# Two Strassen products of eleven blocks computed early and parked in DRAM, in place of four plain blocks

## Chip and metric

One core of one Trainium2 chip. The metric is the device time of one execution in microseconds (us); of several runs, the median. Engines are named as in the profile: PE is TensorE (PEld its weight loads), DVE is VectorE, ACT is ScalarE, POOL is GpSimd, and SP is the queue that issues nearly all DMAs.

## What is computed

One decoder layer on 1024 tokens of width 1024, all in float32: two groups of heads, an output projection, and then a feed-forward part. The change lies in the up-projection of the feed-forward part:

```
h = rms_norm(x, ffn_pre_norm)                          # 1024 x 1024
u = causal_depthwise_conv(h @ w_up, conv_w, conv_b)    # 1024 x 5632, 3 taps over the tokens
u_gate, u_val = split(u)                               # 2 x 2816 columns
y = gelu(u_gate) * u_val
x = x + rms_norm(y @ w_down, ffn_post_norm)
```

## The kernel before

Every float32 matmul is made of three: each operand is split into a high part (a ScalarE copy into a shorter format) and a low part (VectorE takes the difference), and `mm3` (line 121) adds high x high, high x low and low x high into one PSUM bank. A bank is 128 partitions x 512 columns. The tokens are worked on in two halves of 512 (`hh` 0 and 1).

The up-projection has 22 blocks. Block `i` yields 128 gate columns and 128 value columns for all 1024 tokens. Four of them (`AHEAD`) go the plain way: `plain(i, hh)` (line 669) runs 2 x 24 matmuls for each half of the tokens, then the convolution's taps (`taps`, line 660), the gelu and the gate multiply, all 512 wide, and stores the result to `yd` in DRAM. While the plain blocks of the first half run, the second half's residual and norm are made (`post_a`, `post_n`, `post_b`, spread over the units by `interleave`): `post_b` (line 599) transposes the normed rows on TensorE and splits them into `hi` and `lo`. While the plain blocks of the second half run, `tbuild` (line 690) makes the sums of activations T1 to T4 that the other blocks need: it adds high and low parts back together (B), subtracts and splits again.

The other 18 blocks go through Strassen's scheme (`strassen`, line 777): seven products of 12 matmuls instead of eight. Its right operands are T1 to T4 and three quarters of the activations: B11 and B21 (first half of the tokens), B22 (second half). The left operands are made by `prep(i)` (line 729) from the block's weights, loaded into one `raw` tile: four sums on VectorE and seven splits, into the buffers `oh`/`ol` (five each, `split`) and `sh`/`sl` (four each, `ssplit`). The order of products is written out: T1 into bank `PC`, T2 onto bank `PA`, B21 into `PB`, T3 onto `PA`, then `head(i + 1)` (line 770), which opens the next block's `PA` with its B11 product P1, then T4 onto `PA` and B22 onto `PC`. Between the products ScalarE copies `PA` out (`p1`, `u2`, `u3`), and VectorE adds (lines 788, 792, 798) into `ug` and `uv`. `gate(i)` (line 801) then does the taps 1024 wide, the gelu and the multiply, and stores to `yd`.

`prep(i + 1)` stands before `strassen(i)` in the code. A scheduler orders the instructions of each engine when the program is built, by what is ready in its model and by the order in the code; within an engine the result is fixed. `in_turn` (line 94) keeps some of them in the order of the code: the first matmul of every product, and the splits that take a buffer of `oh` or `sh`. Tiles of one tag share a fixed number of buffers: eight of four banks' width for tag T (`ttile`) and eight for tag a (`atile`), four for each of f0 to f3 (`ftile`), two of `xtile`, and three of `u` (`utile`). Four PSUM banks are `big` and four `small`. After the last block the down-projection starts from `load_1` and `feed_1`.

Of the kernel before, what the change touches and what calls it, by code (L numbers as in the profile page):

```python
# [8 lines left out]
F32 = mybir.dt.float32  # L9
# [12 lines left out]
AHEAD = 4  # L22
# [5 lines left out]
def tile_hymba_layer(  # L28
# [61 lines left out]
    yd = dr.tile([NF, P, D], F32, name="yd")  # L90

# [477 lines left out]
    def post_a(hh, b, st):  # L569
        ss = st["ss"][:, b, :]  # L570
        r = norm_cols(ss[:, 0:2], f"post1_{hh}_{b}")
        w = st["wide"]
        tmp = ttile(f"post{hh}_{b}", F32)
        for dh in range(2):
            ds = slice(dh * H, dh * H + H)
            mt = st["m"][b, dh]
            xr = tmp[:, dh, :]
            nc.sync.dma_start(xr, xN[4 * hh + b, :, ds])
            nc.vector.scalar_tensor_tensor(out=mt, in0=mt, scalar=r, in1=w[:, dh, :], op0=ALU.mult, op1=ALU.mult)
            nc.vector.tensor_tensor(out=mt, in0=mt, in1=xr, op=ALU.add)  # L580
        st["h"][b] = tmp

    def post_n(hh, b, st):
        ss = st["ss"][:, b, :]
        w = st["wide"]
        tmp = st["h"][b]
        for dh in range(2):
            ds = slice(dh * H, dh * H + H)
            mt = st["m"][b, dh]
            xr = tmp[:, dh, :]  # L590
            nc.scalar.activation(xr, mt, AF.Square, accum_out=ss[:, 2 + dh : 3 + dh])
            nc.sync.dma_start(x1d[4 * hh + b, :, ds], mt)
        r = norm_cols(ss[:, 2:4], f"pre2_{hh}_{b}")
        for dh in range(2):
            mt = st["m"][b, dh]
            h = tmp[:, 2 + dh, :]
            nc.vector.scalar_tensor_tensor(out=h, in0=mt, scalar=r, in1=w[:, 2 + dh, :], op0=ALU.mult, op1=ALU.mult)

    def post_b(hh, b, st):
        for dh in range(2):  # L600
            ps = small(f"pH{hh}_{b}_{dh}")
            for j in range(4):
                nc.tensor.transpose(ps[:, j * P : j * P + P], st["h"][b][:, 2 + dh, j * P : j * P + P], ident)
            pv = ps.rearrange("p (j q) -> p j q", j=4)
            bs = slice(b * P, b * P + P)
            nc.scalar.activation(st["hi"][dh][:, :, bs], pv, AF.Copy)
            nc.vector.tensor_tensor(
                out=st["lo"][dh][:, :, bs], in0=pv, in1=st["hi"][dh][:, :, bs].bitcast(F32), op=ALU.subtract
            )
# [19 lines left out]
    st_out = []  # L629
    for hh in range(2):  # L630
# [5 lines left out]
        if hh == 0:  # L636
# [7 lines left out]
            def utile(name):  # L644
                return f.tile([P, D], F32, tag="u", name=name, bufs=3)
# [3 lines left out]

            halo = f.tile([P, AHEAD, 2, 2], F32, tag="halo", name="halo")  # L650
            wide = ttile("wide", F32)
            for i in range(2):
                nc.sync.dma_start(wide[:, 2 * i : 2 * i + 2, :], wides[i].rearrange("p (a b) -> p a b", a=2))
# [15 lines left out]
    def plain(i, hh):  # L669
        act = [None, None]  # L670
        for t in range(2):
            b = t * NF + i
            ps = block(w_u[b], act2[hh], f"u{hh}_{i}_{t}")
            u = utile(f"u{hh}_{i}_{t}")
            c0 = 2 * hh
            if hh == 1:
                nc.gpsimd.tensor_copy(u[:, 0:2], halo[:, i, t, :])
            nc.scalar.activation(u[:, c0 : c0 + H], ps, AF.Copy)
            if hh == 0:
                nc.gpsimd.tensor_copy(halo[:, i, t, :], u[:, H - 2 : H])  # L680
            a = ftile(t, f"a{hh}_{i}_{t}")
            taps(a, u, b, c0)
            act[t] = a
        nc.scalar.activation(act[0], act[0], AF.Gelu_apprx_tanh)
        nc.vector.tensor_tensor(out=act[0], in0=act[0], in1=act[1], op=ALU.mult)
        nc.sync.dma_start(yd[i, :, hh * H : hh * H + H], act[0])

    TS = {}

    def tbuild(kt):  # L690
        B = {}
        for n, (hh, k) in (("11", (0, 0)), ("12", (1, 0)), ("22", (1, 1)), ("21", (0, 1))):
            t = ftile(2 + kt % 2, f"B{n}_{kt}")
            hi, lo = act2[hh]
            nc.vector.tensor_tensor(
                out=t, in0=hi[k][:, kt, :].bitcast(F32), in1=lo[k][:, kt, :].bitcast(F32), op=ALU.add
            )
            B[n] = t

        def keep(n, v):  # L700
            if kt == 0:
                TS[n] = (ttile(f"{n}h"), ttile(f"{n}l"))
            h, l = TS[n][0][:, kt, :], TS[n][1][:, kt, :]
            nc.scalar.activation(h, v, AF.Copy)
            nc.vector.tensor_tensor(out=l, in0=v, in1=h.bitcast(F32), op=ALU.subtract)

        def sub(out, x, y, eng):
            eng.tensor_tensor(out=out, in0=x, in1=y, op=ALU.subtract)
            return out

        t1 = sub(B["11"], B["12"], B["11"], nc.vector)
        keep("T1", t1)
        t3 = sub(B["12"], B["22"], B["12"], nc.vector)
        t2 = sub(t1, B["22"], t1, nc.vector)
        keep("T2", t2)
        keep("T3", t3)
        t4 = sub(t2, B["21"], t2, nc.vector)
        keep("T4", t4)

# [9 lines left out]
    def prep(i):  # L729
        if i == AHEAD:  # L730
            raw = [load_w(w_u[t * NF + i], 1024, f"u{i}_{t}") for t in range(2)]
            a11, a12, a21, a22 = [raw[c // 2][:, c % 2 * H : c % 2 * H + H] for c in range(4)]
        else:
            raw = atile(f"raw{i}", F32)
            for t in range(2):
                nc.sync.dma_start(raw[:, 2 * t : 2 * t + 2, :], w_u[t * NF + i].rearrange("p (a b) -> p a b", a=2))
            a11, a12, a21, a22 = [raw[:, c, :] for c in range(4)]
        o = {"B11": split(a11, f"u{i}a11")}
# [29 lines left out]
    heads = {}  # L768

    def head(i):  # L770
        ps = big(f"PA_{i}")
        prod(i, "B11", ps)
        p1 = ftile(2, f"p1_{i}")
        nc.scalar.activation(p1, ps, AF.Copy)
        heads[i] = ps, p1

    def strassen(i):
        pa, p1 = heads.pop(i)
        lo, hi = slice(0, H), slice(H, D)
# [12 lines left out]
        nc.vector.tensor_tensor(out=uv[:, hi], in0=pc, in1=u3, op=ALU.add)  # L792
        if i + 1 < NF:
            head(i + 1)
        prod(i, "T4", pa, first=False)
        nc.scalar.activation(uv[:, lo], pa, AF.Copy)
        prod(i, "B22", pc, first=False)
        nc.vector.tensor_tensor(out=ug[:, hi], in0=pc, in1=u2, op=ALU.add)
        return ug, uv

    def gate(i, ug, uv):
        a = []
        for t, u in enumerate((uv, ug)):
            a.append(wtile(f"a{t}_{i}"))
            taps(a[t], u, (1 - t) * NF + i, 0, D)
# [222 lines left out]
    prep(AHEAD)  # L1028
    head(AHEAD)
    for i in range(AHEAD, NF):  # L1030
        if i + 1 < NF:
            prep(i + 1)
# [4 lines left out]
        gate(i, *strassen(i))  # L1037
# [95 lines left out]
```

## Time and profile before

| | us |
|---|---|
| median of 3 runs (1086.4 to 1087.78) | 1086.94 |
| the profiled execution | 1086.6 |
| its span, first to last instruction | 1084.9 |
| PE busy in the span | 1065.2 |
| DVE busy | 841.6 |
| ACT busy | 586.2 |
| POOL busy | 134.4 |

Times inside the profile count from the start of the span. The end of a matmul is modelled, and neighbours overlap in the records, so the distance between starts tells the pace. A bracket at the end of a timeline row says how long the engine sat idle before that instruction and what ended the wait.

### The profile page before, as it was taken

What the parts mean: (1) busy time and instruction counts of PE and PEld (TensorE: products, weight loads), DVE (VectorE), ACT (ScalarE), POOL (GpSimd) and SP (SyncE); (2) the same over time, 40 slices, a digit from 0 to 9 for tenths busy, and PEclk for the clock granted to TensorE, in tenths of its full rate; (3) what the DMA queues carried; (4) which work ended last, traced back from release to release, by engine and by line L of the source; (5) the groups of instructions that cost most, each with busy time, mean ns of one, the idle gap of its engine ahead of it and who ended that gap; (6) DMA issues with size and microseconds to landing.
All of it is one profiled execution on the core that took longest, in us unless ns stands there. A gap on an engine that the chain in (4) does not pass through costs nothing.

```text
span 1084.9 us, 14366 instructions
## 1 busy us (share of the span) xinstructions
PE 1065.2 (98%) x5052; PEld 897.2 (83%) x5052; DVE 841.6 (78%) x1455; ACT 586.2 (54%) x1130; POOL 134.4 (12%) x139
## 2 busy tenths in 40 slices
PE   8999999999999999998999999999999999999995
PEld 6988998988988888887788888888888788888884
DVE  5567778668677677999887877878777799868687
ACT  6566762476643557667445545455454545544471
POOL 1013332124323111153000000000000000000011
PEclk9999999999999999999999999999999999999999
DMA  8322551321231573334222131221211685634663
GB/s 289 132 78 61 173 170 45 97 73 59 74 107 43 194 268 135 118 125 157 87 82 94 61 114 59 82 94 65 111 59 49 252 290 185 233 98 165 234 203 135
DMA packets 50120, 139.71 MB, mean 129 GB/s; under 512 B 5888, under 2 KB 6016, under 8 KB 50048
## 3 DMA queue, kind: packets, MB, share of 16 engines
q1 hardware_dynamic: 48896, 136.70, 36.9%
q10 hardware_dynamic: 1152, 2.10, 0.5%
q8 instruction: 39, 0.64, 0.2%
q14 instruction: 33, 0.27, 0.1%
HBM read 118.86 MB, written 19.92 MB: 128 GB/s over the span
## 4 chain that ended last, share of the span: by engine, by line
PE 84%; DVE 7%; DMA 3%; ACT 2%; issue 2%; POOL 1%; SPq 0%; DVEq 0%; POOLq 0%; ACTq 0%
PE PA L122 6%; PE PA L124 6%; PE PA L123 6%; PE pd L123 5%; PE pd L124 5%; PE pd L122 5%; PE PC L124 3%; PE PC L122 3%; PE PC L123 3%; PE ps_r L122 3%; PE ps_r L123 3%; PE ps_r L124 3%; PE po L122 3%; PE po L124 3%; PE po L123 3%; PE pn L122 2%
## 5 line engine op out<-in xcount | busy, mean ns | idle before, releaser
L124 PE MATMUL pd<-oh_d,sl_d 128*128 128x512 f32 x264 | 102.7, 389 | 0.0
L123 PE MATMUL pd<-ol_d,sh_d 128*128 128x512 f32 x264 | 102.7, 389 | 0.0
L122 PE MATMUL pd<-oh_d,sh_d 128*128 128x512 f32 x264 | 102.7, 389 | 0.0
L951 POOL TENSOR_TENSOR fs<-fs,mhalf 128x1 f32<-128x1 f32 x8 | 5.8, 731 | 572.0 <-DVE fs L950 572.0
L122 PE MATMUL pn<-oh_n,xh 128*128 128x384 f32 x192 | 65.8, 343 | 0.2 <-DVE gp L284 0.2
L124 PE MATMUL pn<-oh_n,xl 128*128 128x384 f32 x192 | 64.5, 336 | 0.0
L123 PE MATMUL pn<-ol_n,xh 128*128 128x384 f32 x192 | 64.3, 335 | 0.0
L664 DVE SCALAR_TENSOR_TENSOR a<-uv,cvp,a 128x1023 f32<-128x1023 f32 (+1 forms) x36 | 46.0, 1278 | 22.8 <-ACT a L661 22.8
L122 PEld LDWEIGHTS pd<-oh_d,sh_d 128*128 128x128 f32 x264 | 49.6, 188 | 10.4
L123 PEld LDWEIGHTS pd<-ol_d,sh_d 128*128 128x128 f32 x264 | 49.6, 188 | 10.3
L124 PEld LDWEIGHTS pd<-oh_d,sl_d 128*128 128x128 f32 x264 | 49.6, 188 | 10.1
L122 PE MATMUL ps_r<-xh,oh_r 128*128 128x512 f32 x128 | 50.7, 396 | 0.0
L122 PE MATMUL ps_u<-hh,oh_u 128*128 128x512 f32 x128 | 50.0, 390 | 0.0
L123 PE MATMUL ps_r<-xl,oh_r 128*128 128x512 f32 x128 | 50.0, 390 | 0.0
L124 PE MATMUL ps_r<-xh,ol_r 128*128 128x512 f32 x128 | 49.9, 390 | 0.0
L124 PE MATMUL ps_u<-hh,ol_u 128*128 128x512 f32 x128 | 49.8, 389 | 0.0
L123 PE MATMUL ps_u<-hl,oh_u 128*128 128x512 f32 x128 | 49.8, 389 | 0.0
L664 DVE SCALAR_TENSOR_TENSOR a<-ug,cvp,a 128x1023 f32<-128x1023 f32 (+1 forms) x36 | 46.1, 1280 | 2.0
L330 ACT ACTIVATE s<-s,sc,r 128x128 f32<-128x128 f32 x64 | 31.0, 487 | 29.6 <-DVE sc L324 29.6
L113 ACT ACTIVATE oh_o<-wr_o 128x512 fp32r<-128x512 f32 x32 | 19.9, 633 | 38.4 <-PE po L124 37.2
L723 ACT ACTIVATE sh_d<-r 128x512 fp32r<-128x512 f32 x33 | 20.8, 631 | 36.2 <-PE pd L123 23.2
L113 ACT ACTIVATE oh_n<-wr_n 128x384 fp32r<-128x384 f32 x48 | 24.3, 523 | 29.1 <-PE ps_q L123 10.5
(1121 smaller groups left out, 3290.7 us busy)
## 6 DMA issues: line engine op xcount, KB each, us to landing
raw<-w_u SPq DMA_DIRECT2D x34, 512.0 KB, 4.3
r<-yd SPq DMA_DIRECT2D x22, 512.0 KB, 5.6
wr_n<-w_inN SPq DMA_DIRECT2D x24, 384.0 KB, 3.1
wr_u<-w_u SPq DMA_DIRECT2D x18, 512.0 KB, 3.3
yd<-a SPq DMA_DIRECT2D x18, 512.0 KB, 2.6
wr_r<-w_inT SPq DMA_DIRECT2D x16, 512.0 KB, 3.3
wr_o<-w_o SPq DMA_DIRECT2D x16, 512.0 KB, 3.5
wr_d<-w_d SPq DMA_DIRECT2D x11, 512.0 KB, 4.3
```

Source lines behind the costliest of these rows:

```text
L113: in_turn("oh", nc.scalar.activation(hi[:, :n], src, AF.Copy))
L122: ins = nc.tensor.matmul(ps, lh, rh, start=first, stop=False, skip_group_check=onto)
L123: nc.tensor.matmul(ps, lh, rl, start=False, stop=False, skip_group_check=onto)
L124: nc.tensor.matmul(ps, ll, rh, start=False, stop=end, skip_group_check=onto)
L330: nc.scalar.activation(s[:, i, :], s[:, i, :], AF.Exp, scale=r8, bias=c[:, 1, i : i + 1], accum_out=c[:, 3, i : i + 1])
L664: nc.vector.scalar_tensor_tensor(out=a[:, s:], in0=u[:, c0 + s - d : c0 + n - d], scalar=cvp[:, b, tap : tap + 1], in1=a[:, s:], op0=ALU.m ...
L723: in_turn("sh", nc.scalar.activation(hi, src, AF.Copy))
L951: nc.gpsimd.tensor_tensor(out=ss[:, 2:3], in0=ss[:, 3:4], in1=mhalf[:, 0:1], op=ALU.pow)
```

## The change

Blocks 0 to 10 (`EARLY` = 11) get two of their seven products early, while the second half's residual and norm are made: `early(i)` computes P1 (B11) and copies it out, then adds the B21 product onto the same bank and copies P1 + P2, and stores both to a new DRAM tensor `ud`. Only activations of the first half are needed for that. The plain blocks are gone, and all 22 blocks go through `strassen`, in the order 11, 0, 12, 1, ..., 21, 10. For a block below 11, `prep` loads P1 (`seeds`) and P1 + P2 (into `ug`) back; `head` copies P1 into the PSUM bank with ScalarE and adds the T2 product onto it, and `strassen` runs the four that remain. `tbuild` is gone: `post_b` of the second half makes T1 to T4 straight from the transposes, with float32 copies of the first half's (`BF`) that ScalarE keeps. `raw` moves from tag a to tag T, T4 from T to a, and `u` is replaced by two buffers `ug` and one `uv`. The diff, cut to its core:

```diff
-AHEAD = 4
+EARLY = 11
+    ud = dr.tile([EARLY, P, D], F32, name="ud")
...
     def post_b(hh, b, st):
-        for dh in range(2):
-            ps = small(f"pH{hh}_{b}_{dh}")
-            for j in range(4):
-                nc.tensor.transpose(ps[:, j * P : j * P + P], st["h"][b][:, 2 + dh, j * P : j * P + P], ident)
...
+        bs = slice(b * P, b * P + P)
+        if hh == 0:
+            for dh in range(2):
+                pv = turned(hh, b, dh, st)
+                keep((st["hi"][dh], st["lo"][dh]), bs, pv)
+                nc.scalar.activation(BF[dh][:, :, bs], pv, AF.Copy)
+            return
...
+        p12, p22 = [turned(hh, b, dh, st) for dh in range(2)]
+        t1, t2 = [xtile(f"t{n}_{b}").rearrange("p (j q) -> p j q", j=4) for n in (1, 2)]
+        b11, b21 = [BF[dh][:, :, bs] for dh in range(2)]
+        sub(t1, p12, b11)
+        sub(t2, p22, t1)
+        keep(TS["T1"], bs, t1)
+        keep((st["hi"][1], st["lo"][1]), bs, p22)
+        sub(b11, t2, b11)
+        sub(b21, b21, t2)
+        keep(TS["T2"], bs, t2)
+        keep(TS["T3"], bs, b11)
+        keep(TS["T4"], bs, b21)
...
+                for dh in range(2):
+                    BF[dh] = ttile(f"B{dh}", F32)
...
+                for n in range(1, 5):
+                    TS[f"T{n}"] = [(ttile, atile)[n == 4](f"T{n}{c}") for c in "hl"]
...
-            def utile(name):
-                return f.tile([P, D], F32, tag="u", name=name, bufs=3)
+            def gtile(name):
+                return f.tile([P, D], F32, tag="ug", name=name, bufs=2)
+
+            def vtile(name):
+                return f.tile([P, D], F32, tag="uv", name=name, bufs=1)
...
-    def plain(i, hh):
...
-    def tbuild(kt):
...
     def prep(i):
-        if i == AHEAD:
-            raw = [load_w(w_u[t * NF + i], 1024, f"u{i}_{t}") for t in range(2)]
...
+        raw = ttile(f"raw{i}", F32)
...
+        ug[i] = gtile(f"ug{i}")
+        if i < EARLY:
+            seeds[i] = ftile(2, f"p1_{i}")
+            nc.sync.dma_start(seeds[i], ud[i, :, 0:H])
+            nc.sync.dma_start(ug[i][:, 0:H], ud[i, :, H:D])
         else:
-            raw = atile(f"raw{i}", F32)
...
+            o["B11"] = split(a11, f"u{i}a11")
...
+        if i < EARLY:
+            o["T2"] = ssplit(s2, f"u{i}s2")
+            o["T1"] = ssplit(s1, f"u{i}s1")
+        else:
+            o["T1"] = ssplit(s1, f"u{i}s1")
+            o["T2"] = ssplit(s2, f"u{i}s2")
+            o["B21"] = split(a12, f"u{i}a12")
...
+    def early_load(i):
+        raw = load_w(w_u[i], 1024, f"e{i}")
+        ops[i] = {x: split(raw[:, c * H : c * H + H], f"e{i}_{c}") for c, x in enumerate(("B11", "B21"))}
+
+    def early_tail(i):
+        ps, u = heads.pop(i)
+        prod(i, "B21", ps, first=False)
+        nc.scalar.activation(u[:, hi], ps, AF.Copy)
+        nc.sync.dma_start(ud[i], u)
+
+    def early(i):
+        if i < EARLY:
+            early_load(i)
+            ps = big(f"PE_{i}")
+            prod(i, "B11", ps)
+            u = (vtile if i % 3 == 2 else gtile)(f"e{i}")
+            nc.scalar.activation(u[:, lo], ps, AF.Copy)
+            heads[i] = ps, u
+        if i > 0:
+            early_tail(i - 1)
 
     def head(i):
         ps = big(f"PA_{i}")
...
+        u = ftile(2, f"h{i}")
+        if i < EARLY:
+            nc.scalar.activation(ps, seeds.pop(i), AF.Copy)
+            prod(i, "T2", ps, first=False)
+        else:
+            prod(i, "B11", ps)
+        nc.scalar.activation(u, ps, AF.Copy)
+        heads[i] = ps, u
+
+    def strassen(i, then):
+        pa, u = heads.pop(i)
+        g, v = ug.pop(i), vtile(f"uv{i}")
         pc = small(f"PC_{i}")
         prod(i, "T1", pc)
...
+        u2 = u
+        if i >= EARLY:
+            prod(i, "T2", pa, first=False)
+            u2 = ftile(2, f"u2_{i}")
+            nc.scalar.activation(u2, pa, AF.Copy)
+            pb = (small, big)[i % 2](f"PB_{i}")
+            prod(i, "B21", pb)
+            nc.vector.tensor_tensor(out=g[:, lo], in0=pb, in1=u, op=ALU.add)
         prod(i, "T3", pa, first=False)
         u3 = ftile(2, f"u3_{i}")
         nc.scalar.activation(u3, pa, AF.Copy)
...
-        if i + 1 < NF:
-            head(i + 1)
+        if then is not None:
+            head(then)
...
-    interleave([(plain, i, 0) for i in range(AHEAD)], post_stages(1, st_out[1], wide), SPAN1)
+    interleave([(early, i) for i in range(EARLY + 1)], post_stages(1, st_out[1], wide), SPAN1)
     act2[1] = (st_out[1]["hi"], st_out[1]["lo"])
-    interleave([(plain, i, 1) for i in range(AHEAD)], [(tbuild, kt) for kt in range(4)], 0.9)
...
-    prep(AHEAD)
-    head(AHEAD)
-    for i in range(AHEAD, NF):
-        if i + 1 < NF:
-            prep(i + 1)
+    order = [i for c in range(EARLY) for i in (EARLY + c, c)]
+    prep(order[0])
+    head(order[0])
+    for i, then in zip(order, order[1:] + [None]):
+        if then is not None:
+            prep(then)
```

## Rows read from the trace of the kernel before

**Rows 1.** The page, part 1: engine totals over the span.
```profile
PE 1065.2 (98%) x5052; PEld 897.2 (83%) x5052; DVE 841.6 (78%) x1455; ACT 586.2 (54%) x1130; POOL 134.4 (12%) x139
```
**Rows 2.** Timeline of TensorE: first plain matmul, first of the loop (start, length).
```profile
418.24 0.39 PE L122 MATMUL ps_u<-hh,oh_u 128*128 128x512 f32 x1
...
508.82 0.39 PE L122 MATMUL PA<-hh,oh_u4a 128*128 128x512 f32 x1
```
**Rows 3.** Groups by line on TensorE, 418.2 to 511: the transposes.
```profile
L603 PE MATMUL pH<-ident,post 128*128 128x128 f32 x32 | 3.8, 272 | 0.0
```
**Rows 4.** Timeline of TensorE: first product of blocks 11 and 12.
```profile
652.54 0.40 PE L122 MATMUL PC<-T1h,sh_u11s 128*128 128x512 f32 x1
...
671.88 0.40 PE L122 MATMUL PC<-T1h,sh_u12s 128*128 128x512 f32 x1
```
**Rows 5.** Busy time by stretches.
```profile
core 0: us, PE busy (x) PEld busy (x) DVE busy (x) ACT busy (x) POOL busy (x), PEclk, DMA share, GB/s
700.00:800.00 100.00, 100.00 (x436) 81.51 (x435) 78.38 (x101) 50.24 (x73) 0.00 (x0) 1.00 0.23 85
418.20:508.80 90.60, 90.60 (x417) 75.48 (x417) 87.67 (x153) 60.39 (x112) 34.23 (x23) 1.00 0.40 134
485.00:508.80 23.80, 23.80 (x106) 19.71 (x105) 23.80 (x39) 14.85 (x25) 11.66 (x4) 1.00 0.42 135
511.50:520.13 8.63, 5.42 (x14) 3.54 (x14) 8.44 (x14) 4.93 (x9) 0.00 (x0) 0.80 0.35 138
376.00:410.00 34.00, 34.00 (x160) 28.33 (x159) 24.82 (x49) 17.82 (x42) 3.58 (x6) 1.00 0.73 242
857.00:862.00 5.00, 4.21 (x18) 3.30 (x18) 5.00 (x9) 2.92 (x6) 0.00 (x0) 1.00 1.01 356
```
**Rows 6.** Timeline of TensorE where the loop begins.
```profile
511.32 0.39 PE L124 MATMUL PA<-hh,ol_u4a 128*128 128x512 f32 x1
...
513.91 0.50 PE L122 MATMUL PC<-T1h,sh_u4s 128*128 128x512 f32 x1 [2.21 <-ACT sh_u4s L723]
...
516.88 0.63 PE L122 MATMUL PC<-T1h,sh_u4s 128*128 128x512 f32 x1
...
519.86 0.43 PE L123 MATMUL PC<-T1l,sh_u4s 128*128 128x512 f32 x1
...
520.13 0.39 PE L124 MATMUL PC<-T1h,sl_u4s 128*128 128x512 f32 x1
```
**Rows 7.** Groups by line on VectorE, 418.2 to 511.5.
```profile
L664 DVE SCALAR_TENSOR_TENSOR a<-u,cvp,a 128x512 f32<-128x512 f32 (+2 forms) x30 | 22.3, 744 | 0.0
...
L695 DVE TENSOR_TENSOR B<-hh,hl 128x512 f32<-128x512 f32 x16 | 10.6, 684 | 0.0
```
**Rows 8.** Timeline of VectorE in the loop: neighbours back to back.
```profile
655.97 1.28 DVE L664 SCALAR_TENSOR_TENSOR a<-ug,cvp,a 128x1023 f32<-128x1023 f32 x1
657.17 0.68 DVE L724 TENSOR_TENSOR sl_u12s<-raw,sh_u12s 128x512 fp32r<-128x512 f32 x1
657.77 1.28 DVE L664 SCALAR_TENSOR_TENSOR a<-ug,cvp,a 128x1022 f32<-128x1022 f32 x1
```
**Rows 9.** Timeline of VectorE: its first step of the second half's residual.
```profile
415.56 0.16 DVE L566 TENSOR_TENSOR t_post<-ssq 128x1 f32<-128x1 f32 x1 [0.60 <-ACT msq L561]
```
**Rows 10.** The page, part 6: weight loads of the loop.
```profile
raw<-w_u SPq DMA_DIRECT2D x34, 512.0 KB, 4.3
```
**Rows 11.** Timeline of ScalarE while block 10 runs.
```profile
641.44 0.63 ACT L113 ACTIVATE oh_u12a<-raw 128x512 fp32r<-128x512 f32 x1 [0.59 <-PE PB L123]
644.20 0.63 ACT L723 ACTIVATE sh_u11s<-raw 128x512 fp32r<-128x512 f32 x1 [2.13 <-PE PA L123]
644.74 0.58 ACT L791 ACTIVATE u<-PA 128x512 f32<-128x512 f32 x1
```
**Rows 12.** Timeline of TensorE in the last block.
```profile
858.01 0.51 PE L122 MATMUL PA<-T4h,oh_u21a 128*128 128x512 f32 x1 [0.79 <-ACT u L791]
```
**Rows 13.** Timeline of TensorE: the head of block 11.
```profile
644.23 0.40 PE L122 MATMUL PA<-hh,oh_u11a 128*128 128x512 f32 x1
```

More of the change, by code (lines that the diff above doesn't have):

```diff
@@ L572, in post_a @@
         w = st["wide"]
-        tmp = ttile(f"post{hh}_{b}", F32)
+        if hh == 0:
+            tmp = ttile(f"post{hh}_{b}", F32)
+            st["h"][b] = [tmp[:, c, :] for c in range(4)]
+        else:
+            st["h"][b] = [ftile(c // 2, f"post{hh}_{b}_{c}") for c in range(4)]
         for dh in range(2):
@@ L585, in post_n @@
         w = st["wide"]
-        tmp = st["h"][b]
         for dh in range(2):
@@ L595, in post_n @@
             mt = st["m"][b, dh]
[L596 to L609 removed]
+            h = st["h"][b][2 + dh]
@@ new lines, in post_n, with turned, keep @@
+            nc.vector.scalar_tensor_tensor(out=h, in0=mt, scalar=r, in1=w[1][:, dh * H : dh * H + H], op0=ALU.mult, op1=ALU.mult)
+    BF, TS = {}, {}
+    def turned(hh, b, dh, st):
+        ps = small(f"pH{hh}_{b}_{dh}")
+        for j in range(4):
+            nc.tensor.transpose(ps[:, j * P : j * P + P], st["h"][b][2 + dh][:, j * P : j * P + P], ident)
+        return ps.rearrange("p (j q) -> p j q", j=4)
+    def keep(pair, bs, v):
+        h, l = pair[0][:, :, bs], pair[1][:, :, bs]
+        nc.scalar.activation(h, v, AF.Copy)
+        nc.vector.tensor_tensor(out=l, in0=v, in1=h.bitcast(F32), op=ALU.subtract)
@@ new lines, in post_b, with sub @@
+    def post_b(hh, b, st):
+        bs = slice(b * P, b * P + P)
+        if hh == 0:
+            for dh in range(2):
[3 more added lines that the diff above has]
+            return
+        def sub(out, x, y):
+            nc.vector.tensor_tensor(out=out, in0=x, in1=y, op=ALU.subtract)
+            return out
+        p12, p22 = [turned(hh, b, dh, st) for dh in range(2)]
[10 more added lines that the diff above has]
+        keep(TS["T4"], bs, b21)
@@ L642, in ttile @@
                 return f.tile([P, 4, H], dt, tag="T", name=name, bufs=8)
-            def utile(name):
-                return f.tile([P, D], F32, tag="u", name=name, bufs=3)
+            def gtile(name):
+                return f.tile([P, D], F32, tag="ug", name=name, bufs=2)
+            def vtile(name):
+                return f.tile([P, D], F32, tag="uv", name=name, bufs=1)
             def wtile(name):
                 return f.tile([P, D], F32, tag="w", name=name, bufs=2)
-            halo = f.tile([P, AHEAD, 2, 2], F32, tag="halo", name="halo")
-            wide = ttile("wide", F32)
+            wide = [wtile(f"wide{i}") for i in range(2)]
             for i in range(2):
-                nc.sync.dma_start(wide[:, 2 * i : 2 * i + 2, :], wides[i].rearrange("p (a b) -> p a b", a=2))
+                nc.sync.dma_start(wide[i], wides[i])
         else:
@@ L667, in taps @@
             )
-    def plain(i, hh):
[L670 to L688, printed above, removed]
-    def tbuild(kt):
[L691 to L718, printed above, removed]
     def ssplit(src, name):
@@ L729, in prep @@
     def prep(i):
-        if i == AHEAD:
-            raw = [load_w(w_u[t * NF + i], 1024, f"u{i}_{t}") for t in range(2)]
-            a11, a12, a21, a22 = [raw[c // 2][:, c % 2 * H : c % 2 * H + H] for c in range(4)]
-        else:
-            raw = atile(f"raw{i}", F32)
[L735 to L738, printed above, removed]
+        raw = ttile(f"raw{i}", F32)
+        for t in range(2):
+            nc.sync.dma_start(raw[:, 2 * t : 2 * t + 2, :], w_u[t * NF + i].rearrange("p (a b) -> p a b", a=2))
+        a11, a12, a21, a22 = [raw[:, c, :] for c in range(4)]
+        o = {}
+        ug[i] = gtile(f"ug{i}")
[3 more added lines that the diff above has]
+            nc.sync.dma_start(ug[i][:, 0:H], ud[i, :, H:D])
+        else:
+            o["B11"] = split(a11, f"u{i}a11")
         s3, s1 = a11, a21
@@ L791, in strassen, with gate @@
         nc.scalar.activation(u3, pa, AF.Copy)
-        nc.vector.tensor_tensor(out=uv[:, hi], in0=pc, in1=u3, op=ALU.add)
-        if i + 1 < NF:
-            head(i + 1)
+        nc.vector.tensor_tensor(out=v[:, hi], in0=pc, in1=u3, op=ALU.add)
+        if then is not None:
+            head(then)
         prod(i, "T4", pa, first=False)
-        nc.scalar.activation(uv[:, lo], pa, AF.Copy)
+        nc.scalar.activation(v[:, lo], pa, AF.Copy)
         prod(i, "B22", pc, first=False)
-        nc.vector.tensor_tensor(out=ug[:, hi], in0=pc, in1=u2, op=ALU.add)
-        return ug, uv
-    def gate(i, ug, uv):
+        nc.vector.tensor_tensor(out=g[:, hi], in0=pc, in1=u2, op=ALU.add)
+        return g, v
+    def gate(i, g, v):
         a = []
-        for t, u in enumerate((uv, ug)):
+        for t, u in enumerate((v, g)):
             a.append(wtile(f"a{t}_{i}"))
@@ L1036, in tile_hymba_layer @@
             feed(0)
-        gate(i, *strassen(i))
+        gate(i, *strassen(i, then))
     ready = 1
```

38 lines of the change are left out of this document (13 added, 25 removed).

## The prediction

> **What bounds the kernel now.** I read the page's engine totals first [rows 1]: TensorE is busy 1065.2 of 1084.9 us, far more than any other engine. Matmul ends are modelled, so the second view is the start times of neighbouring matmuls, which give the true pace. In the stage of the plain blocks, from the first `ps_u` at 418.24 to the first `PA` at 508.82 [rows 2], lie 384 plain matmuls of 512 columns and 32 transposes. The transposes are busy 3.8 us [rows 3], so a plain matmul takes (90.6 - 3.8)/384 = 0.226 us. One block of the Strassen loop runs from 652.54 to 671.88 [rows 4]: 19.34 us for 7 products of 12 matmuls, 0.230 us each.
>
> The third view, busy time by stretches [rows 5], shows who could take over. In the loop (700 to 800) TensorE is busy 100 of 100 us and VectorE 78.4. Around the plain blocks VectorE is busy 87.7 of 90.6 us, and all of the last 23.8, and there TensorE pays at the end: the matmuls stop at 511.32, the next starts at 513.91, because the first operands (`sh_u4s`) come late, and full pace returns at 520.13 [rows 6]. In the 8.58 us from 511.55 (where the next was due) to 520.13 only 13 matmuls start, worth 3.0 us: **this seam costs 5.6 us** today. About 1.6 of it is pace: eight matmuls, 516.88 to 519.86, start 0.43 us apart instead of 0.23 [rows 6]. The granted clock of the stretch is 0.80 [rows 5], a mixture of the two levels 1.2 and 2.4 GHz.
>
> **The change, part by part.** *Matmuls.* Removed: 384 plain ones, 384 x 0.226 = 86.8 us. Added: 11 blocks x 2 early products x 12 = 264, at the same pace 59.7 us. The loop held 18 x 84 = 1512 and will hold 11 x 84 + 11 x 60 = 1584: 72 more, 16.6 us. Sum -10.5 us, for 48 matmuls fewer. The transposes stay. All of TensorE's time is on the path, so this comes out in full if nothing else gets late.
>
> *The seam.* VectorE's work there [rows 7]: one 512-wide operation steps on by 0.60 us when back to back [rows 8], its 684 ns less the overlap of neighbours; a tap, 744 ns, by 0.66. Removed are 32 taps (21.1 us), 8 gate multiplies (4.8), the 48 operations of `tbuild` (28.8) and 10 of 32 weight splits (6.0). `post_b` of the second half grows from 2 to 9 operations for each of 4 blocks: +28, 16.8 us. Net -43.9. From 87.7 us of work in 90.6 it falls to about 44, and some 7 of `prep` of the first loop block, in 63.5. So VectorE no longer holds this stage, and the 5.6 us should go.
>
> What is late next: `raw` of block 11 is now a buffer of tag T, and its eight are full (T1 to T3, B0 and B1) until the last `post_b` has used B0 and B1. By then VectorE has done, from 415.56 [rows 9], four blocks of 2 x 0.66 + 2 x 0.60 + 2 x 0.66 + 9 x 0.60 + 0.3 = 9.5 us and about 16 splits (9.6): 47.7 us. With the 2.9 us that it idles in all of today's stretch [rows 5], the buffer is free at about 466. The load takes 4.3 us [rows 10], the first split on ScalarE and VectorE 1.3: operands at 472. TensorE finishes the early products at 418.24 + 59.7 + 3.8 = 481.7. That is a margin of 9 us; if it goes, TensorE waits and its clock falls as at 511. The bounds are 0 and the 5.6 of today; I put 1 us, nearer the end that the margin speaks for.
>
> *Loads and stores.* Out go 16 weight loads of 512 KB and 8 stores of 256 KB; in come 11 loads and 11 stores of 512 KB early, and in the loop 8 loads of 512 KB, 22 of 256 KB and 4 stores of 512 KB. Early that is some 15.7 MB with the residual rows, in 63.5 us, 247 GB/s; the stretch 376 to 410 moves 242 GB/s with TensorE full [rows 5]. In the loop 85 GB/s become about 110. Nothing for it. All are issued on SP, where a parked result waits for a ScalarE copy; behind it stand weight loads, whose five split buffers give a lead of 2.5 units of 5.4 us. POOL loses its halo copies and is off the path.
>
> *The loop.* An early block has 60 matmuls, 13.8 us, and a late one 19.3: a pair 33.2. VectorE does 15.2 us for a block today (78.4 of 100 us [rows 5]); an early block saves two splits and one sum, 1.8 us, so a pair has 28.6, or 86%. But it is uneven. In an early block's 13.8 us fall the gate of the late block before it (four taps and a multiply, 1024 wide, 1.20 each [rows 8]: 6.0), `prep` of the late block after it (11 x 0.60 = 6.6) and two sums: 13.8 us. The late block's 19.3 has 13.2. The split buffers hold work about one block ahead, three to six products (8 to 16 us), which carries this over; today's TensorE is full here [rows 5]. Bounds: 0, and 2.0 us a pair, if VectorE's idle time of today (19.3 - 15.2 = 4.1 a block, mostly waits for ScalarE) also comes in each short block and half of it is not carried: 22 us. I take 1 us, since the nearest row is this very loop without a wait.
>
> *The seed copy.* Today a head opens its bank with a matmul; for an early block ScalarE must first copy P1 into the bank. No row shows a copy from SBUF into PSUM; the nearest are 0.58 us (`u` from PSUM to SBUF) and 0.63 (SBUF to SBUF) [rows 11]. In the code it stands behind `u3`, which waits for TensorE. But the code's order is not the engine's: block 12's first split runs at 641.44, ahead of block 10's `u3` at 644.74 [rows 11], because its input was ready. The seed is loaded a block ahead, and ScalarE idles 2.13 us just before. So I expect the copy to go early and cost 0; the other end is the first rival.
>
> *The exit.* The last block is now short: VectorE needs the gate 6.0, two sums 1.2, leftover splits 1.8 and the first feed of the down-projection 4.8 (8 x 0.60), 13.8 us in 13.8. Today's last block loses 0.8 us [rows 12]. Buffers for the first loads come free a few us earlier (`raw` has their tag). Bounds -0.8 and +4; I take +1.
>
> Sum: -10.5 - 5.6 + 1 + 1 + 1 = -13.1. The profiled execution took 1086.6 us (0.3 below the median 1086.94), so **1073.5 us**, 1.2% less.
>
> **The rivals.** *A, slower: the seed copy stays behind `u3`* on ScalarE. Then, at the end of product T3 of every late block, TensorE waits for `u3` and the copy before the early head's T2. In the loop of before the head starts at 644.23 [rows 13]; T3's last matmul ends 0.16 later, `u3` starts at 644.74, behind one split [rows 11], and two copies from there end at about 645.9. That is 1.7 us, 11 times, 18 us; without the split 1.35, 15 us. It decides from 13.1/11 = 1.2 us a pair upwards. Gives 1088 to 1092. For it: the order in the code. Against: rows 11.
>
> *B: VectorE falls behind in the short blocks.* 13.8 us of work in 13.8 leaves no room for its waits on ScalarE; at 0.5 to 1.3 us a pair, 5 to 14 us. Gives 1078 to 1088. For it: VectorE's full stretch before 508.8 did end in waits. Against: the average of 86% and the buffers.
>
> *C: the early seam stays as dear as today,* since T1 to T4 or `raw` of block 11 come after 481.7. Then 5 to 9 us return: 1078 to 1082.
>
> *D: each new wait is paid twice,* because matmuls run at the lower level behind it. The 3 us of my sum become 6: 1076.5. For it: after 511, where a pause of 2.4 us was followed by eight slow matmuls [rows 6]. Against: at 858, behind a wait of 0.79 us [rows 12], the granted clock is 1.00 [rows 5], and my waits are short. The Trainium skill, "TensorE: Matmul & The Clock Gate", Part 1 (The HAM clock gate), says that half rate is the default and that activity releases it; the trace agrees at 511 and not at 858.
>
> **How the numbers follow.** The forecast has 0.60, its own range 1070 to 1077 (no new wait anywhere gives 1070.5). D has 0.05, C 0.08, B 0.16, A 0.11. The range 1069.5 to 1084 holds the forecast but for 0.02, D, C and 0.6 of B: 0.81. A measurement of this kernel can tell 0.2% from no change, 2.2 us: 1084.8 to 1089.1 is "same". Faster: 0.60 + 0.05 + 0.08 + 0.7 of B = 0.84. Same: a quarter of B and a little of A, 0.05. Slower: 0.11.
>
> **What would show it.** Right: 48 matmuls fewer; pairs of loop blocks 33.2 us apart; no TensorE wait of a `PA` for the seed copy, and that copy ahead of `u3`; VectorE under 85% busy between 418 and 480, and a clock of 1.00 there. Wrong: waits of `PA` at every early head (A), of `PC` or `PA` on `sh`, `sl` or `ol` in the loop (B), or a pause near 480 (C), with a clock below 1.00 behind short pauses (D).

## The result, and the profile after

The changed kernel takes 1077.29 us (median of 4 runs), beside 1087.17 of the kernel before in the same session: a ratio of 0.9906, 95% interval 0.9879 to 0.9934. It is faster by 0.9%, and the forecast of 1073.5 was 3.8 us too low, inside its range. The four runs lie between 1073.74 and 1079.47, so a term of 1 us can't be read from times alone; what follows reads the profiled execution, which took 1077.63 us. Of the runs of the experiments one in experiment 3 (1313.28 us, granted clock 0.752) and one in experiment 5 (1327.38, 0.75) fell in a slower state and are left out of the times given. The profiled execution's engine totals, against [rows 1]:

```profile
PE 1051.2 (98%) x5004; PEld 886.6 (82%) x5004; DVE 829.6 (77%) x1428; ACT 587.2 (55%) x1140; POOL 103.9 (10%) x123
```

48 matmuls fewer, 5052 to 5004, as the diff says. Where the three stages begin is read from TensorE's timeline (start, length), as in [rows 2]: the first early product, the last one, the first of the loop, the first of the down-projection.

```profile
418.35 0.39 PE L123 MATMUL PE<-hh,oh_e 128*128 128x512 f32 x1
...
481.60 0.39 PE L125 MATMUL PE<-hh,ol_e 128*128 128x512 f32 x1
481.83 0.39 PE L123 MATMUL PA<-hh,oh_u11a 128*128 128x512 f32 x1
...
852.39 0.39 PE L123 MATMUL pd<-oh_d,sh_d 128*128 128x512 f32 x1
```

The last early matmul starts 0.23 us before the loop's first, one matmul's distance: there is no seam left. By stretches, against [rows 5]:

```profile
core 0: us, PE busy (x) PEld busy (x) DVE busy (x) ACT busy (x) POOL busy (x), PEclk, DMA share, GB/s
...
460.00:482.00 22.00, 22.00 (x102) 18.18 (x101) 18.90 (x32) 13.64 (x27) 0.00 (x0) 1.00 0.67 233
482.00:520.00 38.00, 38.00 (x169) 31.45 (x169) 27.65 (x39) 21.04 (x32) 0.00 (x0) 1.00 0.47 156
...
600.00:700.00 100.00, 97.78 (x426) 79.37 (x425) 80.97 (x105) 52.69 (x78) 0.00 (x0) 1.00 0.31 111
700.00:800.00 100.00, 96.60 (x422) 78.65 (x422) 78.62 (x101) 51.57 (x76) 0.00 (x0) 1.00 0.31 106
```

In the loop TensorE is no longer full: 97.78 and 96.60 of 100 us, where it had 100. The waits between 481.8 and 852.4 (engine, line, what ended the wait: us in total, times, longest) say what it and VectorE waited for:

```profile
DVE raw L732 <- DMA raw<-w_u: 37.1, 12, 4.9
...
PE PA L123 <- ACT u L808: 5.8, 7, 2.3
...
ACT oh_u17a L114 <- DMA raw<-w_u: 4.7, 1, 4.7
```

Before, neither engine waits for `raw` in the loop. TensorE's own entry names ScalarE, but the first row is the one to read. The chain that ended last shows how they hang together, from block 5's last use of its weights to the next waits (start, length, what ran):

```profile
666.46 0.61 DVE sl_u5s L713
...
667.08 0.33 SPq L721
667.42 0.05 issue
667.47 4.32 DMA raw<-w_u
671.83 0.04 issue
671.87 0.70 DVE raw L732
...
680.47 0.61 DVE sl_u17s L713
681.10 3.83 DMA raw<-w_u
684.98 0.51 issue
...
688.96 0.68 DVE sl_u17s L713
689.64 0.30 DVE ug L821
```

The load for block 6 goes out 0.02 us after `sl_u5s`, the last reader of the old contents, and takes 4.32 us, while VectorE stands still for 3.01 us of them:

```profile
671.87 0.69 DVE L732 TENSOR_TENSOR raw<-raw 128x512 f32<-128x512 f32 x1 [3.01 <-DMA raw<-w_u]
```

The load for block 18 does the same behind `sl_u17s` at 680.47. VectorE's adds are queued behind, and on ScalarE behind those stands what TensorE needs:

```profile
690.28 1.25 ACT L701 ACTIVATE a<-ug,cvp 128x1024 f32<-128x1024 f32 x1 [2.04 <-DVE ug L821]
691.43 0.61 ACT L712 ACTIVATE sh_u6s<-s 128x512 fp32r<-128x512 f32 x1
691.95 0.62 ACT L712 ACTIVATE sh_u6s<-raw 128x512 fp32r<-128x512 f32 x1
692.47 0.57 ACT L808 ACTIVATE u<-PA 128x512 f32<-128x512 f32 x1
692.95 0.58 ACT L792 ACTIVATE PA<-p 128x512 f32<-128x512 f32 x1
```

The copy `u` of line 808 waits behind the gate's tap, which waited for `ug`. TensorE's next product, T3 onto the same bank, starts at 693.10, late by a wait of only 0.20 us. At the same place of the next late block the wait is the longest of the loop:

```profile
728.35 0.50 PE L123 MATMUL PA<-T3h,sh_u18s 128*128 128x512 f32 x1 [2.31 <-ACT u L808]
```

The last of the ScalarE rows, at 692.95, is the seed copy: it stands ahead of the T3 copy, and TensorE never waits for it. At the exit two short waits remain, against one of 0.79 us in [rows 12]:

```profile
846.38 0.50 PE L123 MATMUL PA<-T4h,oh_u10a 128*128 128x512 f32 x1 [0.98 <-ACT u L814]
...
855.54 0.50 PE L123 MATMUL pd<-oh_d,sh_d 128*128 128x512 f32 x1 [0.95 <-DVE ug L821]
```

The two spans differ by 1084.9 - 1075.6 = 9.3 us. By stages: the plain or early stage went from 90.58 us (508.82 - 418.24) to 63.48, **-27.1**; the loop from 354.83 (863.65 - 508.82) to 370.56, **+15.7**; the down-projection from 221.25 to 223.2, **+2.0**; what lies ahead, +0.1. The loop takes a second look. The distances of neighbouring matmuls are 0.2303 us in the old loop and 0.2267 in the new one. So the old loop was 1512 x 0.2267 = 342.8, pace 1512 x 0.0036 = 5.4, seam 5.6 and the exit 1.1. The new one is 1584 x 0.2267 = 359.1, 11.1 us of longer distances, nearly all waits and the restarts behind them, and 0.4 of small ones. On the books the change brings 48 matmuls (-10.9), the seam (-5.6), the old exit (-1.1) and, unforeseen, a better pace (-5.4). It gives back 11.5 us in the loop and 2.0 in the down-projection; the sum, -9.5, is within 0.2 of the spans' difference. Pace and waits hang together, as experiment 3 shows.

### The profile page after: what moved, and what is told of

Its sections match the earlier page's. It is cut to its first block, busy times and chain, and to the rows that moved or that the text cites. A ratio compares the mean times of both kernels' runs of the same rounds, so it can differ in the third digit from the quotient of the medians.

```text
span 1075.6 us, 14268 instructions
## 1 busy us (share of the span) xinstructions
PE 1051.2 (98%) x5004; PEld 886.6 (82%) x5004; DVE 829.6 (77%) x1428; ACT 587.2 (55%) x1140; POOL 103.9 (10%) x123
## 4 chain that ended last, share of the span: by engine, by line
PE 63%; DVE 17%; DMA 9%; issue 6%; ACT 4%; POOL 1%; SPq 0%; DVEq 0%; POOLq 0%; ACTq 0%
DMA raw<-w_u 6%; DVE a L704 6%; PE pd L123 5%; PE pd L124 5%; PE pd L125 5%; PE ps_r L123 3%; PE ps_r L125 3%; PE ps_r L124 3%; PE po L123 3%; PE po L125 3%; PE po L124 3%; PE pn L123 2%; PE pn L124 2%; PE pn L125 2%; PE PA L123 2%
## 5 line engine op out<-in xcount | busy, mean ns | idle before, releaser
L704 DVE SCALAR_TENSOR_TENSOR a<-uv,cvp,a 128x1023 f32<-128x1023 f32 (+1 forms) x44 | 56.2, 1277 | 9.5 <-ACT a L701 9.5
L704 DVE SCALAR_TENSOR_TENSOR a<-ug,cvp,a 128x1023 f32<-128x1023 f32 (+1 forms) x44 | 56.2, 1277 | 0.5 <-ACT a L701 0.5
L701 ACT ACTIVATE a<-ug,cvp 128x1024 f32<-128x1024 f32 x22 | 27.4, 1246 | 38.0 <-DVE ug L821 35.7
L732 DVE TENSOR_TENSOR raw<-raw 128x512 f32<-128x512 f32 x22 | 15.2, 689 | 37.5 <-DMA raw<-w_u 37.5
L829 ACT ACTIVATE a<-a 128x1024 f32<-128x1024 f32 x22 | 23.4, 1062 | 36.2 <-DVE a L704 36.2
L114 ACT ACTIVATE oh_n<-wr_n 128x384 fp32r<-128x384 f32 x48 | 24.3, 523 | 28.7 <-PE ps_q L124 10.3
```

The lines of the kernel that those rows point to most:

```text
L114: in_turn("oh", nc.scalar.activation(hi[:, :n], src, AF.Copy))
L701: nc.scalar.activation(a, u[:, c0 : c0 + n], AF.Identity, scale=cvp[:, b, 2:3], bias=cvp[:, b, 3:4])
L704: nc.vector.scalar_tensor_tensor(out=a[:, s:], in0=u[:, c0 + s - d : c0 + n - d], scalar=cvp[:, b, tap : tap + 1], in1=a[:, s:], op0=ALU.m ...
L732: nc.vector.tensor_tensor(out=s3, in0=a11, in1=a21, op=ALU.subtract)
L829: nc.scalar.activation(a[1], a[1], AF.Gelu_apprx_tanh)
```

## The experiments

**1. Where do the loop's waits come from?** Theory L: `raw` has two buffers, and a load can only go out when the block two before has been read. Theory V (rival B): VectorE has too much to do in the short blocks. The early blocks' weights go to the three `wr` buffers, half the size and idle in the loop (a block needs two), so the two `raw` buffers serve late blocks alone:

```diff
-        raw = ttile(f"raw{i}", F32)
...
+        if i < EARLY:
+            raw = [load_w(w_u[t * NF + i], 1024, f"u{i}_{t}", True) for t in range(2)]
+            a11, a12, a21, a22 = [raw[c // 2][:, c % 2 * H : c % 2 * H + H] for c in range(4)]
+        else:
+            raw = ttile(f"raw{i}", F32)
...
```

(`True` keeps the loads of `wr` in the order of the code, the down-projection's too.)

> Edit: the weights of blocks 0 to 10 are loaded by prep into the small weight buffers wr (two of three), so that the two raw buffers of tag T serve the late blocks alone; nothing else. Theory L (the weights land late): the loop's TensorE waits (11.1 us beyond the pace in the changed kernel) come from VectorE and ScalarE standing in order before a raw tile that is still being loaded (37 us of VectorE's waits in the loop). With more buffers the loads start earlier: VectorE's waits for raw fall under 10 us, TensorE's waits in the loop under 4 us, time 1068 to 1071 where the changed kernel has 1077. Theory V (VectorE simply has too much work in a short block, rival B of the prediction): the loads come early, VectorE's waits for them go, but TensorE still waits 9 us or more; 1076 to 1078.

Measured: **1067.31 us**, ratio 0.9818 (0.9804 to 0.9831). It beats both kernels. VectorE's waits for these weights, and two stretches of the loop:

```profile
DVE wr_u L738 <- DMA wr_u<-w_u: 4.2, 10, 0.6
```

```profile
600.00:700.00 100.00, 100.00 (x442) 82.78 (x442) 84.15 (x107) 56.17 (x80) 0.00 (x0) 1.00 0.32 111
700.00:800.00 100.00, 100.00 (x443) 82.80 (x442) 85.80 (x110) 55.57 (x79) 0.00 (x0) 1.00 0.33 111
```

VectorE's 37.1 us of waits for weights become 4.2 (and 0.3 for `raw`), TensorE is full in these stretches, and VectorE does the same work at 84 to 86% without holding anyone. L holds and V falls. The Trainium skill, "Trainium Kernel Development and Optimization", Best Practices, asks for two buffers, to overlap transfers with compute. Two were there, and in this case that was not enough: TensorE had been busy for 97.78 and 96.60 of 100 us with them.

**2. Is it SP's queue instead?** The loads of the parked results move from SP to POOL's queue, and the weight loads on SP have nothing ahead of them but stores:

```diff
-            nc.sync.dma_start(seeds[i], ud[i, :, 0:H])
-            nc.sync.dma_start(ug[i][:, 0:H], ud[i, :, H:D])
+            nc.gpsimd.dma_start(seeds[i], ud[i, :, 0:H])
+            nc.gpsimd.dma_start(ug[i][:, 0:H], ud[i, :, H:D])
```

> Edit: the two loads that bring the parked products back (22 of 256 KB) are issued on the POOL queue instead of SP. Theory Q (the queue): on SP the load into ug waits for the last tap of the gate two blocks before, and the weight loads stand behind it; taken off SP they start earlier, VectorE's waits for raw fall by a third or more, time 1071 to 1074. Theory L (buffers): the weight loads wait for the raw buffer itself (its last reader is the split of T3), so nothing changes: 1076 to 1079, VectorE's waits for raw 30 to 40 us.

Measured: 1090.29 us, ratio 1.0032 (1.0019 to 1.0045), slower than the kernel before; neither theory gave this time. VectorE still waits 38.3 us for `raw` (37.5 in the whole changed kernel), so SP's queue was not the cause. The loop now takes 382.5 us and has 22.9 us over the pace, of which 13.6 are TensorE's waits. The seeds land later (ScalarE waits 12.3 us for them, 4 times; in the changed kernel 1.4 us, once). Behind some of TensorE's waits come matmuls at half pace:

```profile
767.81 0.54 PE L123 MATMUL PA<-T3h,sh_u19s 128*128 128x512 f32 x1 [1.84 <-ACT u L808]
...
768.57 0.63 PE L125 MATMUL PA<-T3h,sl_u19s 128*128 128x512 f32 x1
768.99 0.63 PE L123 MATMUL PA<-T3h,sh_u19s 128*128 128x512 f32 x1
769.42 0.63 PE L124 MATMUL PA<-T3l,sh_u19s 128*128 128x512 f32 x1
```

```profile
765.00:772.00 7.00, 5.16 (x16) 3.81 (x15) 7.00 (x8) 4.82 (x7) 0.00 (x0) 0.76 0.00 0
```

Starts are 0.43 us apart at a granted clock of 0.76, a mixture of the levels 1.2 and 2.4 GHz. That is the mechanism of rival D, which the changed kernel doesn't show at its own waits. The Trainium skill, "TensorE: Matmul & The Clock Gate", Part 1 (The HAM clock gate), puts the full rate down to activity, and the rows above agree with it. The length of a wait alone doesn't decide here: the one of 1.95 us at 697.89 in the same run is followed by full pace (granted clock 1.00 from 697 to 704). How much of the 12 us more in the loop comes from POOL's queue itself was not separated.

**3. Does the pace hang on where the tiles lie?** Before, the feed-forward tiles start behind the `halo` tile of 64 bytes, which the change drops. Without it they start on multiples of 256 bytes, and the tiles of tags a, f0 to f3, `oh` and `ol` do so in every version. First the halo was made 128 bytes long (its unused half is never touched), and 64 bytes were put ahead in the changed kernel:

```diff
-            halo = f.tile([P, AHEAD, 2, 2], F32, tag="halo", name="halo")
+            halo = f.tile([P, 2 * AHEAD, 2, 2], F32, tag="halo", name="halo")
```

> Edit: the kernel before with its halo tile 128 bytes a partition instead of 64, so that every tile that follows it in the pool begins at a multiple of 128 bytes instead of 64 beyond one; the instructions are the same in the same order. Theory P (place in memory): in the loop of the kernel before a matmul steps on by 0.2303 us, everywhere else and in the whole changed kernel by 0.2267, because of that shift; 1512 matmuls x 0.0036 = 5.4 us: the pace becomes 0.2267 and the time 1081 to 1083. Rival (the pace belongs to the loop's own order or traffic): 0.2303 and 1086 to 1088.

> Edit: the changed kernel with a 64-byte tile put in front of the pool of the feed-forward stage, so that its tiles begin 64 bytes beyond a multiple of 128, as in the kernel before. Theory P: the loop's pace becomes 0.2303; 1584 matmuls x 0.0036 = 5.7 us slower, less what of it falls into today's waits: 1079 to 1083. Rival: pace 0.2267, 1076 to 1079.

Measured: 1088.39 us, ratio 1.0011 (1.0002 to 1.002), loop pace 0.2307; and 1076.68, ratio 0.9906 (0.9892 to 0.9921), loop pace 0.2292. So 64 bytes cost the changed kernel 0.0025 us a matmul, and its time doesn't show it: what stands over the common pace is 5.9 us in place of 11.1, since TensorE comes later to the same late weights (VectorE's waits for `raw` stay at 37.7 us). In the changed kernel, then, the better pace by itself gains nothing that these intervals can tell. On 128 bytes the old loop gains nothing. The same 64 bytes in the version of experiment 1, where no wait hides them:

> The version with three buffers, with an unused tile of 64 bytes ahead of the tiles of the feed-forward part. There the loop's TensorE waits for nothing up to 800 us, so a slower pace can't hide in waits. Theory P: the placement sets the pace, 0.2292 in place of 0.2267 us a matmul as in the other shifted kernel, 1584 x 0.0025 = 4 us: 1070 to 1072.5. Rival: the pace there came with the waits, and with no waits it stays 0.2267: 1066 to 1068.5.

Measured: 1072.1 us, ratio 0.9865 (0.9849 to 0.9882), 4.8 us more, at 0.2292 a matmul: theory P. Then one group of tiles alone was moved, with 64 bytes ahead of the T tiles and 192 behind them, and in reverse:

```diff
                     BF[dh] = ttile(f"B{dh}", F32)
+                pad1 = f.tile([P, 48], F32, tag="pad1", name="pad1")
+                nc.vector.memset(pad1, 0.0)
...
+            pad0 = f.tile([P, 16], F32, tag="pad0", name="pad0")
+            nc.vector.memset(pad0, 0.0)
```

(The second part runs first.)

> The version with three buffers; 64 bytes ahead of the T tiles and 192 behind them, so that the T tiles (the T operands, the late blocks' weights) stand 64 bytes off a multiple of 256 and the outputs u, the gate tiles stand on one as before. Theory T: the matmul pace follows the tiles that TensorE reads: 0.229 us a matmul in the loop and 1071 to 1073. Theory R: it follows the tiles that VectorE and ScalarE work on: 0.2267 and 1066 to 1068.5.

> The reverse: the T tiles on a multiple of 256 bytes, the outputs u and the gate tiles 64 bytes off. Theory T: 0.2267 us a matmul and 1066 to 1068.5. Theory R: 0.229 and 1071 to 1073. If this one and the last are both slow, it is no group of tiles alone.

Measured: 1071.63 (ratio 0.9859, 0.9846 to 0.9872) and 1067.54 (0.9819, 0.9805 to 0.9833). The first product of two late blocks, a pair or 144 matmuls apart, with the T tiles moved:

```profile
550.63 0.40 PE L125 MATMUL PC<-T1h,sh_u13s 128*128 128x512 f32 x1
...
583.63 0.40 PE L125 MATMUL PC<-T1h,sh_u14s 128*128 128x512 f32 x1
```

and with the others moved:

```profile
549.59 0.39 PE L125 MATMUL PC<-T1h,sh_u13s 128*128 128x512 f32 x1
...
582.23 0.39 PE L125 MATMUL PC<-T1h,sh_u14s 128*128 128x512 f32 x1
```

33.00 against 32.64 us, 0.2292 against 0.2267 a matmul: it is the T tiles. Last, the kernel before with a halo of 256 bytes, no more than a longer unused end:

```diff
-            halo = f.tile([P, AHEAD, 2, 2], F32, tag="halo", name="halo")
+            halo = f.tile([P, 16, 2, 2], F32, tag="halo", name="halo")
```

> The kernel before with a halo tile of 256 bytes (64 before), no other change: every larger tile then stands on a multiple of 256 bytes, as in the changed kernel; with 128 bytes the pace had stayed at 0.2307. Theory: a start on 256 bytes gives the pace of 0.2267; 1512 loop matmuls x 0.0036 = 5.4 us less, 1081 to 1082.5, ratio 0.995. Rival: the pace hangs on which tile is where, not on the start: 1086 to 1089.

Measured: 1084.47 us, ratio 0.9967 (0.9953 to 0.998). Blocks 11 and 12, as in [rows 4]:

```profile
651.09 0.39 PE L122 MATMUL PC<-T1h,sh_u11s 128*128 128x512 f32 x1
...
670.13 0.39 PE L122 MATMUL PC<-T1h,sh_u12s 128*128 128x512 f32 x1
```

19.04 us in place of 19.34, 0.2267 a matmul. The theory holds for the pace. For the time it was 2 us too hopeful by the median. In the profiled execution a longer wait in the last block (1.84 us in place of 0.79, with seven matmuls at 0.43 behind it) took part of the 5.4 back:

```profile
854.37 0.49 PE L122 MATMUL PA<-T4h,oh_u21a 128*128 128x512 f32 x1 [1.84 <-ACT u L791]
```

The seven runs fall into two groups, three from 1080.87 to 1081.98, about where the theory had them, and four from 1084.47 to 1085.19, the profiled one among them. Whether the slow matmuls of that wait part the two groups no run shows.

**4. What would the seed copy have cost behind the T3 copy?** Rival A, put into the version of experiment 1 by one edge between the two copies:

```diff
-            nc.scalar.activation(ps, seeds.pop(i), AF.Copy)
+            in_turn("seed", nc.scalar.activation(ps, seeds.pop(i), AF.Copy))
...
-        nc.scalar.activation(u3, pa, AF.Copy)
+        in_turn("seed", nc.scalar.activation(u3, pa, AF.Copy))
```

> The version with the early blocks' weights in three buffers (1067.31 us), with one edge more: ScalarE may make a seed copy only after the T3 copy of the block before. Rival A's price, the copies on TensorE's path: the late block's T3 ends, its copy out 0.57 us, then the seed copy 0.59 us, each with its hand-over, 1.3 to 1.7 us of TensorE wait in each of 11 late blocks, so 15 to 18 us: 1082 to 1086. If TensorE finds other work in that time, or the seed copy is not what it needs next, nothing to 3 us: 1067 to 1070.

Measured: 1088.97 us, ratio 1.0011 (1.0 to 1.0023), 21.7 us above experiment 1. TensorE's waits in the loop, and one of the eleven places, on ScalarE and TensorE:

```profile
PE PA L125 <- ACT PA L798: 16.5, 11, 1.8
```

```profile
564.98 0.63 ACT L714 ACTIVATE sh_u2s<-wr_u 128x512 fp32r<-128x512 f32 x1 [2.08 <-PE PA L126]
565.51 0.58 ACT L820 ACTIVATE u<-PA 128x512 f32<-128x512 f32 x1
565.99 0.59 ACT L798 ACTIVATE PA<-p 128x512 f32<-128x512 f32 x1
```

```profile
566.64 0.50 PE L125 MATMUL PA<-T2h,sh_u2s 128*128 128x512 f32 x1 [1.47 <-ACT PA L798]
```

A split, the T3 copy, the seed copy, then TensorE: the order that rival A described. Each place costs 1.47 us of wait and 0.27 of restart (starts 1.86 and 0.34 apart where 0.227 is due), 19.1 us in eleven. Behind the last one eight matmuls run 0.43 us apart, 1.6 us. That is more than the expectation had, and one choice in ScalarE's order would have used up the whole gain of the version of experiment 1.

**5. Did VectorE's relief remove the seam?** Work was given back to VectorE in the early stage of the version of experiment 1, as subtractions whose result nobody reads. At first they read nothing but their own tile:

```diff
+            for _ in range(2):
+                nc.vector.tensor_tensor(out=fill, in0=fill, in1=fill, op=ALU.subtract)
```

> The version with three buffers and two idle 128x512 subtractions on VectorE in each of the 11 early blocks (22 at 0.61 us, 13.4 us more in a stretch of 64 us in which VectorE is busy for 57). Theory: the seam was VectorE's backlog and its relief removed it; then 13.4 less the 6.6 us that are free come back as a wait ahead of the first loop products, about 5 to 8 us: 1072 to 1075, with TensorE's wait between 470 and 490 us. Rival: the seam hung on buffers or loads, and this changes nothing: 1066 to 1069.

Measured: 1069.6 us, ratio 0.9839 (0.9825 to 0.9854). This tested nothing. The rows of that tile (engine, operation, count: durations, first and last start) say why:

```profile
L794 DVE TENSOR_TENSOR fill<-fill x22: 677/689/693, 365.4 to 412.3; 128x512 f32<-128x512 f32 x22
```

All 22 ran before the stage began, since nothing held them. So each was tied to the low halves that its block makes:

```diff
+        for x in ("B11", "B11", "B21", "B21"):
+            nc.vector.tensor_tensor(out=fill, in0=ops[i][x][1].bitcast(F32), in1=fill, op=ALU.subtract)
```

> The version with three buffers, again with idle subtractions on VectorE in the early stage, four of 0.61 us in each of the 11 early blocks (26.8 us), and now each reads a low half that the block has just made, so that it can't run ahead of its block. Theory: VectorE's relief removed the seam. With 26.8 us more, VectorE can't end the operand sums at 469 us, but 15 to 25 us later; TensorE then waits ahead of the first T products or in the early products, 8 to 20 us in all: 1075 to 1088. Rival: the operand sums are wanted so late that 25 us cost nothing, and the seam had another cause: 1066 to 1070.

Measured: 1088.29 us, ratio 1.0004 (0.9993 to 1.0015), 21.0 us above experiment 1. TensorE's waits and one stretch of the early stage:

```profile
PE PE L127 <- DVE ol_e L117: 11.9, 4, 4.9
```

```profile
460.00:482.00 22.00, 16.04 (x49) 11.51 (x50) 20.37 (x36) 9.42 (x17) 0.54 (x1) 0.71 0.23 75
```

The loop begins at 502.90 in place of 481.73. With 26.8 us more of it, VectorE's work sets the end of this stage again. The loss sits in the early products, not at one seam, and it is dearer than the waits: of 24.3 us over the pace between 418 and 500 (2.6 between 418 and 480 in experiment 1), 12.6 are waits, and much of the rest is half pace; the granted clock of the stretch shown is 0.71. Ahead of the longest wait VectorE works back to back, subtractions and operand sums by turns, from 454.74 us to the low half that TensorE waits for (462.55), so the order in its queue counts beside the amount. That the old seam itself came from VectorE's backlog fits this and its full 23.8 us ahead of the seam [rows 5], but no run changed VectorE's work alone in the kernel before.

**6. The last wait.** In the version of experiment 1 TensorE waits once in the loop, 1.80 us in its last block, behind ScalarE. A late block was put last:

```diff
+    order[-2:] = order[-1], order[-2]
```

> The version with three buffers, with the last two blocks changed over, so that a late block (7 products) ends the loop in place of an early one. Theory: the wait of 1.8 us in the last block and the slow matmuls behind it (8 at 0.43 in place of 0.227 us, 1.6 us) come from ScalarE, which waits 4 us for the gate of the block before with the T3 copy queued behind; a longer last block lets the gate pass first: 3 us less, 1063.5 to 1065. Rival: the wait moves to the end of the late block or to the down-projection's first operands: 1066.5 to 1068.5.

Measured: 1068.92 us, ratio 0.9836 (0.9822 to 0.9851): no gain. The wait goes over into four shorter places (1.2, 0.5 and 0.7 us in all), one of them in front of the down-projection: the rival's reading.

## Why the prediction came out as it did

The direction and the range were right. Three terms hold, one was mis-sized, and one was missing; that the last two partly cancel was not foreseen.

*Matmuls, -10.5.* Right: 48 x 0.2267 = 10.9. The early stage was to end at 481.7 and ended at 481.83.

*The seam, -5.6 and +1 for a new one.* The 5.6 us went and no new one came, so rival C and the +1 did not come true. That VectorE's work can hold this stage is shown by experiment 5; that it alone made the old seam is argued from its full stretch. The working was less good than the result: VectorE was to be busy for some 51 of 63.5 us and was for 57 (19.06, 19.42 and 18.90 between 418 and 482). One sign of being right failed with it: VectorE was to be under 85% busy between 418 and 480, and it was busy for 91% (56.57 of 62 us).

*The seed copy, 0.* Right, and for the reason given: it is issued ahead of the T3 copy. A's price was 1.35 to 1.7 us a place, and experiment 4 measured 1.74.

*The loop's waits, +1.* **This step failed**: 11.1 us, of it 1.7 in the last block. With a pace of 0.2292 it was about half (5.9 us, experiment 3), still several times the term. Two blocks, forecast to take 33.2 us, took 32.64 where no wait fell and up to 35.58 with one. The prediction bounded the term with 0 and 22 and took the low end because "the nearest row is this very loop without a wait". It looked for the limit in VectorE's work alone, and there it was right: 86% was forecast, and experiment 1 shows 84 to 86% with TensorE full. What it left out is the buffer. It followed when `raw` comes free for block 11, once, and not for the blocks after it; of the loads it said "nothing for it", by bandwidth. A load of 4.3 us [rows 10] behind the last reader was hidden in blocks of 19.3 us with two buffers. With the same two and blocks of 13.8 and 19.3 by turns it was not. So the rival that came nearest, B, had the right place and symptom and the wrong cause.

*The exit, +1.* About right: 0.98 and 0.95 us of wait in place of 0.79. The second stands in the down-projection, whose +2.0 it half explains; the rest was not followed up.

*A term that was missing, -5.4.* The pace of the loop. The prediction took 0.226 and 0.230 us a matmul as two facts and priced the loop at the second. The difference came from the 64 bytes of `halo`, which the change removed by the way. Against the waits it cancels in part. In the loop, apart from matmuls and seam, 11.1 + 0.4 - 5.4 - 1.1 (the old exit) = 5.0 us came on top, and 2.0 in the down-projection: 7.0, where loop and exit together had 2. Less the 1 for a seam that didn't come and the 0.3 that the matmuls gave on top, this is 3.7 of the 3.8 us by which the spans' -9.3 misses the -13.1. The profiled execution's 4.1 (1077.63 - 1073.5) holds 0.3 more from outside the span.

*D* was wrong for this kernel and right as a mechanism: in experiments 2 and 5 some waits were paid nearly twice, in the profiled execution of the changed kernel none.

## What to carry over

When a loop's steps become shorter or uneven, redo for every tile the sum of last reader, transfer and first use: a buffer count that was enough for steps of 19 us was not for steps of 19 and 14 by turns, and the wait showed up two engines further on, under another name. Compare the distance of neighbouring matmuls between kernels before and after, since a changed pace hides in a sum that is priced by counts. And give an experiment's added work an input from its own stage, or it runs somewhere else.

## Not expected of the hardware

In this loop the pace of 512-column matmuls depends on where tiles start in SBUF. With the T tiles on a multiple of 256 bytes it was 0.2267 us, and 64 bytes off 0.2292. In the kernel before, with all of the larger feed-forward tiles moved together, it was 0.2303 at 64 bytes, 0.2307 at 128 and 0.2267 at 256. It holds for the loop alone: the down-projection of the same kernels runs at 0.2267, and the plain products of the kernel before, which read `hh` as the loop does, at 0.2268. In the loop it also holds for products whose own tiles were not moved (those with `hh`: 0.2308 at 64 bytes, 0.2280 at 128, 0.2267 at 256). Why those slow down too stays open. Nor was it tried which of the tiles under tag T does it in the changed kernel, the operands T1 to T3 or the weights in `raw`; in the kernel before it can't be `raw`, which lay under tag a and did not move.
